# A transformer kernel's two FFNs in panels of 1024 columns, with two of eight pairs of k tiles as seven block products

## The chip, the core and the metric

The kernel runs on one core of one Trainium2 chip. Its time is the device time of one execution in microseconds (us), and the figure used is the median of several runs.

## What is computed

Two blocks in a row work on 256 tokens of 2048 numbers. Each begins with its own mixers (state space and sparse attention in the first; gated delta net and sparse attention in the second), which the change leaves alone. Each ends in the same FFN, 2048 to 8192 and back, in float32:

```python
u = rmsnorm(x, g_mlp) @ w_up
return x + jnp.square(jax.nn.relu(u)) @ w_down
```

## The kernel before

Every large product with a weight goes through `panel`. It makes a panel of 512 output columns for all 256 tokens (two token tiles, t = 0 and 1, one PSUM bank each, tiles `mm0` and `mm1`). The activations are the stationary operand, transposed, 128 of the 2048 contracted numbers (one k tile) by 128 tokens; the weights are streamed. To keep float32 accuracy with the float32r format, both operands are split in a high and a low part, and each product is three matmuls: high by high (L192), high by low (L193), low by high (L194).

Weights come in loads of 1 MB (`wst`, three buffers) on SP's queue (L201). For every 128 x 1024 elements ACT writes the high part `whi` (L207) and DVE then the low part `wlo` (L208). Each has four buffers; one holds the weights of 12 matmuls, and a buffer is free again when these 12 are done.

`ffn` (L266) has four stages of 2048 hidden columns. A stage makes four up panels and four down panels of 512 columns. After an up panel ACT takes the ReLU out of PSUM (`u`, L276), DVE squares it (L277), PE transposes it in eight steps into two `tp` banks (L287), and `split` (L170 on ACT, L172 on DVE) makes the parts `hTh` and `hTl` that the down panels use. After a down panel DVE adds each bank to the residual `X`, scaled by the squared norm factor `rr` (L292). PSUM has eight banks, in four tags of two: `mm0`, `mm1`, `tp`, `sx`. So a panel uses two banks, the next one the other two.

The order on each engine is set when the program is built: a scheduler takes the instructions of the code and interleaves them; at run time each engine follows its list strictly.

## Time and profile before

| What | us |
|---|---|
| median of three runs | 2679.77 |
| lowest and highest run | 2679.11, 2683.38 |
| span of the profiled execution, first to last instruction | 2681.1 |
| busy PE, DVE, ACT in that span | 2661.9, 1551.4, 1245.3 |
| granted TensorE clock, mean | 0.998 of full speed |

The profile gives no separate time of the profiled execution; its span is 1.3 us above the median of the runs. Busy time of PE counts overlapping matmuls once, and a matmul's row is longer than its distance to the next. An idle time in a row is that of the engine just before the instruction, with what ended it.

### The profile page before, as it was taken

The numbers are of one execution on the slowest core, as the hardware profiler recorded it, in microseconds if no ns is written. First come the engines' busy times: TensorE is split into PE (matmuls) and PEld (weight loads), VectorE is DVE, ScalarE is ACT, GpSimd is POOL, SyncE is SP. The second block draws the span as 40 slices with busy tenths as digits, with TensorE's granted clock in tenths as the row PEclk, the third lists the DMA queues.
The fourth block names the chain that finished last, engine by engine and source line by source line (L and its number), as shares of the span: only waits on it lengthen the run. The fifth ranks groups of instructions, "written<-read, shape, count | busy, mean of one in ns | idle before, by whom it ended". The sixth has DMA issues, their size and how long they took to land.

```text
span 2681.1 us, 31989 instructions
## 1 busy us (share of the span) xinstructions
PE 2661.9 (99%) x12836; PEld 2223.4 (83%) x12836; DVE 1551.4 (58%) x2023; ACT 1245.3 (46%) x1622; POOL 38.3 (1%) x46
## 2 busy tenths in 40 slices
PE   8999999999999999999999999999999999999998
PEld 8988888888888888888888877888888888888887
DVE  5767755555555555576755866455555555555554
ACT  5555544434444344454533654444444344443443
POOL 0000000000000000000100000000000000000000
PEclk9999999999999999999999999999999999999999
DMA  7444555555555655653422743556555555555564
GB/s 235 152 161 160 181 185 184 189 193 184 189 192 184 195 186 192 204 186 117 141 96 87 268 143 110 189 187 220 188 188 185 193 189 188 188 188 189 188 204 141
DMA packets 253587, 478.61 MB, mean 179 GB/s; under 512 B 9127, under 2 KB 50046, under 8 KB 253438
## 3 DMA queue, kind: packets, MB, share of 16 engines
q1 hardware_dynamic: 247280, 467.57, 52.4%
q10 hardware_dynamic: 6158, 8.99, 1.1%
q8 instruction: 101, 1.65, 0.3%
q14 instruction: 48, 0.39, 0.0%
HBM read 472.32 MB, written 4.21 MB: 178 GB/s over the span
## 4 chain that ended last, share of the span: by engine, by line
PE 98%; ACT 0%; DVE 0%; DMA 0%; issue 0%; ACTq 0%; POOL 0%; POOLq 0%; SPq 0%; DVEq 0%
PE mm L194 29%; PE mm L193 29%; PE mm L192 29%; PE tp L287 1%; PE sx L858 1%; PE sx L853 1%; PE tp L253 1%; PE tp L752 0%; PE sx L1132 0%; PE sx L887 0%; PE sx L392 0%; PE tp L545 0%; PE sx L1164 0%; PE sx L886 0%; PE mm L994 0%; PE sx L823 0%
## 5 line engine op out<-in xcount | busy, mean ns | idle before, releaser
L208 DVE TENSOR_TENSOR wlo<-wst,whi 128x1024 fp32r<-128x1024 f32 (+5 forms) x896 | 1064.0, 1189 | 956.6 <-ACT whi L207 955.4
L207 ACT ACTIVATE whi<-wst 128x1024 fp32r<-128x1024 f32 (+5 forms) x896 | 923.7, 1032 | 1181.8 <-PE mm L194 1168.8
L192 PE MATMUL mm<-whi,xnh 128*128 128x512 f32 (+3 forms) x1440 | 553.6, 385 | 2.0 <-ACT whi L207 1.6
L193 PE MATMUL mm<-wlo,xnh 128*128 128x512 f32 (+3 forms) x1440 | 552.6, 384 | 0.0
L194 PE MATMUL mm<-whi,xnl 128*128 128x512 f32 (+3 forms) x1440 | 549.9, 383 | 0.1
L193 PE MATMUL mm<-wlo,hTh 128*128 128x512 f32 x1024 | 399.4, 390 | 0.0
L192 PE MATMUL mm<-whi,hTh 128*128 128x512 f32 x1024 | 399.3, 390 | 0.0
L194 PE MATMUL mm<-whi,hTl 128*128 128x512 f32 x1024 | 398.8, 389 | 0.0
L192 PEld LDWEIGHTS mm<-whi,xnh 128*128 128x128 f32 x1440 | 270.9, 188 | 48.3 <-ACT whi L207 2.0
L194 PEld LDWEIGHTS mm<-whi,xnl 128*128 128x128 f32 x1440 | 270.9, 188 | 46.3 <-DVE xnl L174 0.4
L193 PEld LDWEIGHTS mm<-wlo,xnh 128*128 128x128 f32 x1440 | 271.3, 188 | 44.2
L193 PE MATMUL mm<-wlo,x2h 128*128 128x512 f32 (+3 forms) x736 | 278.9, 379 | 0.7 <-DVE wlo L208 0.7
L194 PE MATMUL mm<-whi,x2l 128*128 128x512 f32 (+3 forms) x736 | 279.3, 380 | 0.0
L192 PE MATMUL mm<-whi,x2h 128*128 128x512 f32 (+3 forms) x736 | 278.8, 379 | 0.0
L192 PEld LDWEIGHTS mm<-whi,hTh 128*128 128x128 f32 x1024 | 192.3, 188 | 39.7
L194 PEld LDWEIGHTS mm<-whi,hTl 128*128 128x128 f32 x1024 | 192.3, 188 | 39.6
L193 PEld LDWEIGHTS mm<-wlo,hTh 128*128 128x128 f32 x1024 | 192.3, 188 | 39.1
L193 PEld LDWEIGHTS mm<-wlo,x2h 128*128 128x128 f32 x736 | 138.9, 189 | 21.0 <-DVE wlo L208 1.0
L192 PEld LDWEIGHTS mm<-whi,x2h 128*128 128x128 f32 x736 | 138.9, 189 | 20.2 <-issue 1.1
L194 PEld LDWEIGHTS mm<-whi,x2l 128*128 128x128 f32 x736 | 138.8, 189 | 19.9 <-issue 0.9
L276 ACT ACTIVATE u<-mm 128x512 f32<-128x512 f32 x64 | 38.3, 598 | 34.0 <-PE mm L194 31.3
L277 DVE TENSOR_TENSOR u<-u 128x512 f32<-128x512 f32 x64 | 43.9, 692 | 11.3 <-ACT u L276 11.3
(411 smaller groups left out, 2131.9 us busy)
## 6 DMA issues: line engine op xcount, KB each, us to landing
wst<-in_w_up_dram SPq DMA_DIRECT2D x128, 1024.0 KB, 5.4
wst<-in_w_down_dram SPq DMA_DIRECT2D x128, 1024.0 KB, 5.0
wst<-in_w_in_dram SPq DMA_DIRECT2D x84, 1024.0 KB, 4.9
wst<-in_w_out_dram SPq DMA_DIRECT2D x16, 1024.0 KB, 5.0
wst<-in_w_o_dram SPq DMA_DIRECT2D x16, 1024.0 KB, 5.0
wst<-in_w_in_dram SPq DMA_DIRECT2D x16, 780.0 KB, 4.3
wst<-in_w_in_dram SPq DMA_DIRECT2D x12, 824.0 KB, 4.5
wst<-in_w_in_dram SPq DMA_DIRECT2D x12, 736.0 KB, 6.0
```

Source lines behind the costliest of these rows:

```text
L192: PE.matmul(ps[t][:, :n], xh[:, sl], wa, start=kt == first, stop=False)
L193: PE.matmul(ps[t][:, :n], xh[:, sl], wb, start=False, stop=False)
L194: PE.matmul(ps[t][:, :n], xl[:, sl], wa, start=False, stop=kt == last)
L207: S.activation(a[:, :2 * n], src, AF.Copy)
L208: V.tensor_tensor(b[:, :2 * n], src, a[:, :2 * n].bitcast(F32), op=OP.subtract)
L253: PE.transpose(ps[:, kk, t, :], x[:, t, (k0 + kk) * 128:(k0 + kk + 1) * 128], ident)
L276: S.activation(u, ps[t], AF.Relu)
L277: V.tensor_tensor(u, u, u, op=OP.mult)
L287: PE.transpose(pv[:, kk, t, :], us[t][:, c:c + 128], ident)
L853: PE.matmul(ps[:, i * 64:(i + 1) * 64].rearrange("p (m b) -> p m b", b=b), N[:, i], half(T[:, i], 0), start=True, stop=True)
L858: PE.matmul(ps[:, i * 64:(i + 1) * 64].rearrange("p (m b) -> p m b", b=b), P[:, i], half(Tt[:, i], 1), start=True, stop=True)
```

## The change

In both FFNs, `wide` takes the place of `panel` for 1024 columns at once. A load of 1 MB now holds two k tiles by 1024 columns, in rows of 4 KB instead of 2 KB. Each pair of k tiles, with two token tiles and two halves of 512 columns, is a 2 x 2 by 2 x 2 block product. In six of the eight pairs it is done as before by eight products of three matmuls. In pairs 2 and 5 (`SPAIRS`) it is done by seven products, by Winograd's form of Strassen's algorithm: sums of activation blocks (`a_forms`, made once per activation) by sums of weight blocks (`t13`, `t24`, made on DVE for each load). A panel holds eight banks: P2, P3, P4, E take the plain pairs and some of the seven; P1, P5, P6, P7 only take products of pairs 2 and 5, and `shared` adds them up on ACT and DVE. The two groups of tags change roles from panel to panel. The last two 512-column down panels of each FFN stay in the old form, so there are 15 wide panels in an FFN.

After an up panel DVE adds each of P2, P3, P4, E to its shared part (new line L376), ACT takes the ReLU, now with the norm factor as scale (L377), and ACT squares it (L378). The transposes are L390. `s2` has one buffer more.

```diff
@@ -218,6 +218,98 @@
             mms(*m)
         return ps
 
+    SPAIRS = (2, 5)
+    turn = [0]
+    def a_forms(f, forms, j):
+        sf = s2([128, 4, 128], name="sf")
+        V.tensor_tensor(sf[:, 0], f[:, 0, 1], f[:, 1, 1], op=OP.add)
+        V.tensor_tensor(sf[:, 2], f[:, 0, 0], f[:, 0, 1], op=OP.subtract)
+        V.tensor_tensor(sf[:, 1], sf[:, 0], f[:, 0, 0], op=OP.subtract)
+        V.tensor_tensor(sf[:, 3], f[:, 1, 0], sf[:, 1], op=OP.subtract)
+        sh, sl = s2([128, 4, 128], F32R, "sfh"), s2([128, 4, 128], F32R, "sfl")
+        split(flat(sf), flat(sh), flat(sl))
+        forms[j] = sh, sl
+    def wide(w, r0, c0, lhs, forms):
+        ka, kb = (("mm0", "mm1"), ("tp", "sx"))[::1 - 2 * (turn[0] % 2)]
+        turn[0] += 1
+        B = {}
+        for k, names in zip((ka[0], ka[1], kb[0], kb[1]), (("P2", "P3"), ("P4", "E"), ("P1", "P5"), ("P6", "P7"))):
+            for b in names:
+                B[b] = psum(k, [128, 512])
+        ns = len(SPAIRS)
+        left = {b: 3 * ns + (0 if b in ("P1", "P5", "P6", "P7") else 6 * (8 - ns)) for b in B}
+        left["E"] = 6 * (8 - ns)
+        total = dict(left)
+        def mm(b, x, y):
+            PE.matmul(B[b], x, y, start=left[b] == total[b], stop=left[b] == 1)
+            left[b] -= 1
+        def product(b, xh, xl, wa, wb):
+            mm(b, xh, wa)
+            mm(b, xh, wb)
+            mm(b, xl, wa)
+        def parts(src, n=1024):
+            a = whp.tile([128, 1024], F32R, name="whi")
+            b = wlp.tile([128, 1024], F32R, name="wlo")
+            S.activation(a[:, :n], src, AF.Copy)
+            V.tensor_tensor(b[:, :n], src, a[:, :n].bitcast(F32), op=OP.subtract)
+            return [(a[:, o:o + 512], b[:, o:o + 512]) for o in range(0, n, 512)]
+        for j in range(8):
+            s = stp.tile([128, 2048], F32, name="wst")
+            nc.sync.dma_start(s.rearrange("p (k n) -> p k n", k=2),
+                              w[r0 + j * 256:r0 + j * 256 + 256, c0:c0 + 1024].rearrange("(k p) n -> p k n", p=128))
+            if j not in SPAIRS:
+                for kk in range(2):
+                    xh, xl = lhs(2 * j + kk)
+                    wl = parts(s[:, kk * 1024:(kk + 1) * 1024])[::-1]
+                    for i, l, b in ((0, 0, "P2"), (0, 1, "P3"), (1, 0, "P4"), (1, 1, "E")):
+                        h = slice(i * 128, i * 128 + 128)
+                        product(b, xh[:, h], xl[:, h], *wl[l])
+                continue
+            t13 = sp([128, 2, 512], name="t13")
+            V.tensor_tensor(t13, s.rearrange("p (k l n) -> p k l n", k=2, l=2)[:, :, 0],
+                            s[:, :1024].rearrange("p (l n) -> p l n", l=2)[:, ::-1], op=OP.subtract)
+            t24 = sp([128, 2, 512], name="t24")
+            V.tensor_tensor(t24[:, 0], s[:, 1024:1536], t13[:, 0], op=OP.subtract)
+            V.tensor_tensor(t24[:, 1], s[:, 1536:], t24[:, 0], op=OP.subtract)
+            (a1h, a1l), (a2h, a2l) = lhs(2 * j), lhs(2 * j + 1)
+            m1, m2 = slice(0, 128), slice(128, 256)
+            sh, sl = forms[j]
+            def sums(n):
+                return sh[:, n - 1], sl[:, n - 1]
+            w11, w22 = parts(s[:, 512:1536])
+            product("P1", a1h[:, m1], a1l[:, m1], *w11)
+            product("P3", *sums(4), *w22)
+            u1, u3 = parts(flat(t13))
+            product("P5", *sums(1), *u1)
+            product("P7", *sums(3), *u3)
+            u2, u4 = parts(flat(t24))
+            product("P6", *sums(2), *u2)
+            product("P4", a2h[:, m2], a2l[:, m2], *u4)
+            (w21,) = parts(s[:, 1536:], 512)
+            product("P2", a2h[:, m1], a2l[:, m1], *w21)
+        return B, ka
+    def shared(B):
+        p1, u2, u4, v = (s2([128, 512], name=n) for n in ("cp1", "cu2", "cu4", "cv"))
+        S.activation(p1, B["P1"], AF.Copy)
+        V.tensor_tensor(u2, B["P6"], p1, op=OP.add)
+        V.tensor_tensor(u4, B["P5"], u2, op=OP.add)
+        V.tensor_tensor(u2, B["P7"], u2, op=OP.add)
+        V.tensor_tensor(v, B["P5"], u2, op=OP.add)
+        return ((0, 0, p1, B["P2"]), (0, 1, u4, B["P3"]), (1, 0, u2, B["P4"]), (1, 1, v, B["E"]))
...
@@ -244,16 +336,27 @@
             start += z
         return o
 
-    def x_to_act(x, q, gain):
-        """One [128 tokens, 2, 512] panel of x -> [128, 4, 256] transposed, times gain, in two parts."""
+    def x_to_act(x, q, gain, forms=None, p=0):
         for k0 in range(0, 4, 2):
             ps = psum("tp", [128, 512]).rearrange("p (k t c) -> p k t c", k=2, t=2)
             for kk in range(2):
                 for t in range(2):
                     PE.transpose(ps[:, kk, t, :], x[:, t, (k0 + kk) * 128:(k0 + kk + 1) * 128], ident)
+            if forms is not None and 2 * p + k0 // 2 in SPAIRS:
+                f = s2([128, 2, 2, 128], name="ff")
+                for kk in range(2):
+                    S.activation(f[:, kk], ps[:, kk], AF.Copy, scale=gain[:, k0 + kk:k0 + kk + 1])
+                f_to_act(f, q, k0, forms, 2 * p + k0 // 2)
+                continue
             for kk in range(2):
                 k = k0 + kk
                 split(ps[:, kk].rearrange("p t c -> p (t c)"), q[0][:, k], q[1][:, k], gain[:, k:k + 1])
+    def f_to_act(f, q, k0, forms, j):
+        fv = f.rearrange("p k t c -> p (k t c)")
+        split(fv, flat(q[0][:, k0:k0 + 2]), flat(q[1][:, k0:k0 + 2]))
+        a_forms(f, forms, j)
 
     def x_rstd(ssx, name):
         ss = tiny([128, 2], "ssr")
@@ -263,37 +366,57 @@
     def flat(ap):
         return ap.rearrange("p k c -> p (k c)")
 
-    def ffn(X, act, w_up, w_down, r, after, tail=0):
-        rr = tiny([128, 2], "rr")
-        V.tensor_tensor(rr, r, r, op=OP.mult)
+    def ffn(X, act, forms, w_up, w_down, r, after, tail=0):
         for s_ in range(4):
-            hT = []
-            for p in range(4):
-                ps = panel(w_up, 0, 16, s_ * 2048 + p * 512, 512, at_k(act))
-                us = []
-                for t in range(2):
-                    u = s2([128, 512], name=f"u{t}")
-                    S.activation(u, ps[t], AF.Relu)
-                    V.tensor_tensor(u, u, u, op=OP.mult)
-                    us.append(u)
-                q = quarter("hT")
-                hT.append(q)
-                for k0 in range(0, 4, 2):
-                    pt = psum("tp", [128, 512])
-                    pv = pt.rearrange("p (k t c) -> p k t c", k=2, t=2)
-                    for kk in range(2):
+            hT, hforms = [], {}
+            for P in range(2):
+                B, tags = wide(w_up, 0, s_ * 2048 + P * 1024, at_k(act), forms)
+                us = {}
+                for i, l, part, bank in shared(B):
+                    V.tensor_tensor(part, bank, part, op=OP.add)
+                    S.activation(part, part, AF.Relu, scale=r[:, i:i + 1])
+                    S.activation(part, part, AF.Square)
+                    us[i, l] = part
+                for l in (1, 0):
+                    q = quarter("hT")
+                    p = len(hT)
+                    hT.append(q)
+                    for k0 in range(0, 4, 2):
+                        pt = psum(tags[k0 // 2], [128, 512])
+                        pv = pt.rearrange("p (k t c) -> p k t c", k=2, t=2)
+                        for kk in range(2):
+                            for t in range(2):
+                                c = (k0 + kk) * 128
+                                PE.transpose(pv[:, kk, t, :], us[t, l][:, c:c + 128], ident)
+                        j = 2 * p + k0 // 2
+                        if j in SPAIRS:
+                            f = s2([128, 2, 2, 128], name="ff")
+                            S.activation(f.rearrange("p k t c -> p (k t c)"), pt, AF.Copy)
+                            f_to_act(f, q, k0, hforms, j)
+                        else:
+                            split(pt, flat(q[0][:, k0:k0 + 2]), flat(q[1][:, k0:k0 + 2]))
+            for P in range(2):
+                if (s_, P) == (3, 1):
+                    for p in (2, 3):
+                        ps = panel(w_down, s_ * 2048, 16, p * 512, 512, at_k(hT), tail=tail if p == 3 else 0)
                         for t in range(2):
-                            c = (k0 + kk) * 128
-                            PE.transpose(pv[:, kk, t, :], us[t][:, c:c + 128], ident)
-                    split(pt, flat(q[0][:, k0:k0 + 2]), flat(q[1][:, k0:k0 + 2]))
-            for p in range(4):
-                ps = panel(w_down, s_ * 2048, 16, p * 512, 512, at_k(hT), tail=tail if (s_, p) == (3, 3) else 0)
-                for t in range(2):
-                    V.scalar_tensor_tensor(X[p][:, t], ps[t], rr[:, t:t + 1], X[p][:, t], op0=OP.mult, op1=OP.add)
-                    if s_ == 3:
-                        after(p, t)
-
```

The lists of the engines change most where an up panel ends and the next panel begins. In the rows below a tile's name ends in its own number, and `whi_4079` is one buffer's worth of weights.

ACT, end of an up panel, before (the two ReLUs of the panel stand between the splits for the next one):

```order
L207 ACTIVATE whi_3977<-wst_3959 128x1024
L207 ACTIVATE whi_3995<-wst_3993 128x1024
L276 ACTIVATE u0_3935<-mm0_3797 128x512
L276 ACTIVATE u1_3938<-mm1_3798 128x512
L207 ACTIVATE whi_4011<-wst_3993 128x1024
L170 ACTIVATE hTh_3941<-tp_3943 128x512
L170 ACTIVATE hTh_3941<-tp_3950 128x512
L207 ACTIVATE whi_4029<-wst_4027 128x1024
```

and now, at the end of the first up panel (`cp1`, `cu4`, `cu2`, `cv` are the four quarters of u):

```order
L261 ACTIVATE whi_4045<-wst_4027 128x1024
L261 ACTIVATE whi_4063<-wst_4061 128x1024
L377 ACTIVATE cp1_3955<-cp1_3955,r2_3651 128x512
L261 ACTIVATE whi_4079<-wst_4061 128x1024
L378 ACTIVATE cp1_3955<-cp1_3955 128x512
L377 ACTIVATE cu4_3957<-cu4_3957,r2_3651 128x512
L377 ACTIVATE cu2_3956<-cu2_3956,r2_3651 128x512
L378 ACTIVATE cu4_3957<-cu4_3957 128x512
L378 ACTIVATE cu2_3956<-cu2_3956 128x512
L377 ACTIVATE cv_3958<-cv_3958,r2_3651 128x512
L261 ACTIVATE whi_4102<-wst_4095 128x1024
L378 ACTIVATE cv_3958<-cv_3958 128x512
```

Two instructions per 512 columns became eight per 1024, four of which read what another one of ACT has just written, and a split of weights for the next panel stands between the first ReLU and its square, another one ahead of the last square.

DVE at the same place, before:

```order
L208 TENSOR_TENSOR wlo_3996<-wst_3993,whi_3995 128x1024
L277 TENSOR_TENSOR u0_3935<-u0_3935 128x512
L277 TENSOR_TENSOR u1_3938<-u1_3938 128x512
L208 TENSOR_TENSOR wlo_4012<-wst_3993,whi_4011 128x1024
L172 TENSOR_TENSOR hTl_3942<-tp_3943,hTh_3941 128x512
L172 TENSOR_TENSOR hTl_3942<-tp_3950,hTh_3941 128x512
L208 TENSOR_TENSOR wlo_4030<-wst_4027,whi_4029 128x1024
L208 TENSOR_TENSOR wlo_4046<-wst_4027,whi_4045 128x1024
```

and now:

```order
L262 TENSOR_TENSOR wlo_4030<-wst_4027,whi_4029 128x1024
L310 TENSOR_TENSOR cv_3958<-tp_3660,cu2_3956 128x512
L262 TENSOR_TENSOR wlo_4046<-wst_4027,whi_4045 128x1024
L279 TENSOR_TENSOR t13_4097<-wst_4095 128x1024
L376 TENSOR_TENSOR cp1_3955<-mm0_3655,cp1_3955 128x512
L376 TENSOR_TENSOR cu4_3957<-mm0_3656,cu4_3957 128x512
L376 TENSOR_TENSOR cu2_3956<-mm1_3657,cu2_3956 128x512
L376 TENSOR_TENSOR cv_3958<-mm1_3658,cv_3958 128x512
L262 TENSOR_TENSOR wlo_4064<-wst_4061,whi_4063 128x1024
L262 TENSOR_TENSOR wlo_4080<-wst_4061,whi_4079 128x1024
L282 TENSOR_TENSOR t24_4099<-wst_4095,t13_4097 128x512
L283 TENSOR_TENSOR t24_4099<-wst_4095,t24_4099 128x512
```

The two squares are gone. In their place are four adds that read the banks, behind the difference `t13_4097` of the next panel's third load (`wst_4095`).

PE, just after the end of an up panel, before (`mm0_3797`, `mm1_3798` are the next panel):

```order
L192 MATMUL mm1_3798<-whi_3801,xnh_3119 128x512
L287 MATMUL tp_3783<-idt_82,u0_3775 128x128
L287 MATMUL tp_3790<-idt_82,u0_3775 128x128
L193 MATMUL mm1_3798<-wlo_3802,xnh_3119 128x512
L194 MATMUL mm1_3798<-whi_3801,xnl_3120 128x512
L287 MATMUL tp_3783<-idt_82,u1_3778 128x128
L287 MATMUL tp_3783<-idt_82,u0_3775 128x128
L287 MATMUL tp_3783<-idt_82,u1_3778 128x128
L287 MATMUL tp_3790<-idt_82,u1_3778 128x128
L287 MATMUL tp_3790<-idt_82,u0_3775 128x128
L287 MATMUL tp_3790<-idt_82,u1_3778 128x128
L192 MATMUL mm0_3797<-whi_3801,xnh_3119 128x512
```

and now (`tp_4020` is the next panel; five products stand ahead of these rows, and two more and six transposes follow, four of them of `cv` and two of `cu4`):

```order
L250 MATMUL tp_4020<-whi_4045,xnh_3119 128x512
L250 MATMUL tp_4020<-wlo_4046,xnh_3119 128x512
L250 MATMUL tp_4020<-whi_4045,xnl_3120 128x512
L390 MATMUL mm0_3978<-idt_82,cu4_3957 128x128
L390 MATMUL mm1_3985<-idt_82,cu4_3957 128x128
L390 MATMUL mm0_3994<-idt_82,cp1_3955 128x128
L390 MATMUL mm0_3994<-idt_82,cu2_3956 128x128
L390 MATMUL mm0_3994<-idt_82,cp1_3955 128x128
L390 MATMUL mm0_3994<-idt_82,cu2_3956 128x128
L390 MATMUL mm1_4012<-idt_82,cp1_3955 128x128
L390 MATMUL mm1_4012<-idt_82,cu2_3956 128x128
L390 MATMUL mm1_4012<-idt_82,cp1_3955 128x128
```

The first transposes stood behind four matmuls of the next panel; they now stand behind 18.

## Rows read from the trace of the kernel before

**Rows 1.** The page: busy time, granted clock, one group of matmuls.
```profile
PE 2661.9 (99%) x12836; PEld 2223.4 (83%) x12836; DVE 1551.4 (58%) x2023; ACT 1245.3 (46%) x1622; POOL 38.3 (1%) x46
...
PEclk9999999999999999999999999999999999999999
...
L192 PE MATMUL mm<-whi,hTh 128*128 128x512 f32 x1024 | 399.3, 390 | 0.0
```
**Rows 2.** What PE waited for, whole span: total us, times, longest.
```profile
PE tp L141 <- DMA P<-in_g_mix_dram: 5.3, 1, 5.3
PE mm L193 <- DVE wlo L208: 0.7, 1, 0.7
```
**Rows 3.** Timeline of PE, start and us: two matmuls, 54 apart, steady.
```profile
2008.43 0.39 PE L192 MATMUL mm<-whi,xnh 128*128 128x512 f32 x1
...
2020.67 0.39 PE L192 MATMUL mm<-whi,xnh 128*128 128x512 f32 x1
```
**Rows 4.** One up panel with its eight transposes, busy time by engine.
```profile
2004.29:2027.10 22.81, 22.81 (x106) 18.72 (x105) 12.37 (x13) 10.66 (x13) 0.00 (x0) 1.00 0.57 186
```
**Rows 5.** Groups by form on DVE and ACT: xcount | busy us, mean ns.
```profile
L208 DVE TENSOR_TENSOR wlo<-wst,whi 128x1024 fp32r<-128x1024 f32 x776 | 949.9, 1225 | 883.4 <-ACT whi L207 882.5 <-issue 0.2
...
L277 DVE TENSOR_TENSOR u<-u 128x512 f32<-128x512 f32 x64 | 43.9, 692 | 11.3 <-ACT u L276 11.3
...
L172 DVE TENSOR_TENSOR hTl<-tp,hTh 128x512 fp32r<-128x512 f32 x64 | 41.0, 682 | 0.0
...
L838 DVE TENSOR_TENSOR N<-A,C 128x512 f32<-128x512 f32 x20 | 13.7, 684 | 0.0
...
L483 DVE TENSOR_TENSOR NP<-sx,Bt 128x512 f32<-128x512 f32 x8 | 5.5, 685 | 1.1 <-PE sx L1132 0.9
...
L817 DVE SCALAR_TENSOR_TENSOR D<-D,rk,C 128x128 f32<-128x128 f32 x16 | 4.5, 344 | 0.0
...
L207 ACT ACTIVATE whi<-wst 128x1024 fp32r<-128x1024 f32 x776 | 822.3, 1060 | 1064.0 <-PE mm L194 1053.5 <-DMA wst<-in_w_in_dram 3.0 <-issue 2.6
...
L276 ACT ACTIVATE u<-mm 128x512 f32<-128x512 f32 x64 | 38.3, 598 | 34.0 <-PE mm L194 31.3
...
L170 ACT ACTIVATE hTh<-tp 128x512 fp32r<-128x512 f32 x64 | 34.8, 596 | 15.6 <-PE tp L287 15.6
...
L1055 ACT ACTIVATE gsq<-O 128x512 f32<-128x512 f32 x4 | 2.3, 616 | 0.0
...
L1231 ACT ACTIVATE X<-X,r 128x512 f32<-128x512 f32 x2 | 1.4, 724 | 2.1 <-POOL r L159 2.1
```
**Rows 6.** Timeline at the end of an up panel: start, us, engine.
```profile
2002.82 1.28 ACT L276 ACTIVATE u<-mm 128x512 f32<-128x512 f32 x2 [0.98 <-PE mm L194]
...
2003.45 1.37 DVE L277 TENSOR_TENSOR u<-u 128x512 f32<-128x512 f32 x2 [0.35 <-ACT u L276]
...
2003.99 1.06 ACT L207 ACTIVATE whi<-wst 128x1024 fp32r<-128x1024 f32 x1
...
2004.29 0.41 PE L287 MATMUL tp<-idt,u 128*128 128x128 f32 x2
```
**Rows 7.** Timeline inside a panel: matmul, next weight split on ACT, DVE.
```profile
2009.79 0.39 PE L192 MATMUL mm<-whi,xnh 128*128 128x512 f32 x1
...
2009.99 1.06 ACT L207 ACTIVATE whi<-wst 128x1024 fp32r<-128x1024 f32 x1 [1.68 <-PE mm L194]
...
2011.08 1.23 DVE L208 TENSOR_TENSOR wlo<-wst,whi 128x1024 fp32r<-128x1024 f32 x1 [1.51 <-ACT whi L207]
```
**Rows 8.** Weight loads: queue, median us to landing, min/median/max in 2000:2600.
```profile
q1 hardware_dynamic: 247280, 467.57, 52.4%
...
wst<-in_w_up_dram SPq DMA_DIRECT2D x128, 1024.0 KB, 5.4
...
wst<-in_w_down_dram SPq DMA_DIRECT2D x128, 1024.0 KB, 5.0
...
DMA to landing us min/median/max: 4.9/5.4/7.7
```
**Rows 9.** Timeline of ACT: a Copy (L207) and a Square (L167) behind it.
```profile
1957.97 1.06 ACT L207 ACTIVATE whi<-wst 128x1024 fp32r<-128x1024 f32 x1 [1.66 <-PE mm L194]
...
1958.94 0.61 ACT L167 ACTIVATE junk<-X 128x512 bf16<-128x512 f32 x1
```

More of the change, by code (lines that the diff above doesn't have):

```diff
@@ L71, in build @@
     drp = ctx.enter_context(tc.tile_pool(name="drp", bufs=1, space=bass.MemoryType.DRAM))
-    NP, N4, N2, N1 = 7, 17, 15, 5
+    NP, N4, N2, N1 = 7, 17, 16, 5
     def sp(shape, dt=F32, name="sp"):
@@ new lines, in ffn @@
+            for P in range(2):
+                if (s_, P) == (3, 1):
+                    for p in (2, 3):
+                        ps = panel(w_down, s_ * 2048, 16, p * 512, 512, at_k(hT), tail=tail if p == 3 else 0)
+                        for t in range(2):
+                            V.tensor_tensor(X[p][:, t], ps[t], X[p][:, t], op=OP.add)
+                            after(p, t)
+                    continue
+                B, _ = wide(w_down, s_ * 2048, P * 1024, at_k(hT), hforms)
+                out_ = shared(B)
+                for i, l, part, bank in out_:
+                    x = X[2 * P + 1 - l][:, i]
+                    V.tensor_tensor(x, part, x, op=OP.add)
+                for i, l, part, bank in out_:
+                    x = X[2 * P + 1 - l][:, i]
+                    V.tensor_tensor(x, bank, x, op=OP.add)
+                if s_ == 3:
+                    for p in range(2):
+                        for t in range(2):
+                            after(p, t)
@@ L660, in build, with add_panel @@
     ssx = tiny([128, 2, 4], "ssx", bufs=2)
-    def add_panel(ps, p, scale, act, gain, ssx):
+    def add_panel(ps, p, scale, act, gain, ssx, forms):
         for t in range(2):
@@ L665, in add_panel @@
         q = quarter("xn")
-        x_to_act(X[p], q, gain[:, 4 * p:4 * p + 4])
+        x_to_act(X[p], q, gain[:, 4 * p:4 * p + 4], forms, p)
         act.append(q)
@@ L671, in build @@
     X = x_panels()
+    xforms = {}
     for p in range(4):
@@ L689, in after1 @@
             nc.scalar.dma_start(xsave[:, p], X[p])
-    ffn(X, xn, I["w_up"][0], I["w_down"][0], r, after1)
+    ffn(X, xn, xforms, I["w_up"][0], I["w_down"][0], r, after1)
     if upto == 2:
@@ L1199, in build @@
     xn = []
+    xforms = {}
     ssx = tiny([128, 2, 4], "ssx", bufs=2)
@@ L1205, in build @@
         q = quarter("xn")
-        x_to_act(X[p], q, g_ln2[:, 4 * p:4 * p + 4])
+        x_to_act(X[p], q, g_ln2[:, 4 * p:4 * p + 4], xforms, p)
         xn.append(q)
```

4 lines of the change are left out of this document (2 added, 2 removed).

## The prediction

> **What bounds the kernel now.** I read the page first. PE is busy 99% of the span at a granted clock of nine tenths or more in all 40 slices, DVE 58%, ACT 46% [rows 1]. A busy PE need not be a limiting one, since a matmul's row (390 ns) overlaps the next. So the second view is what PE waited for: the longest wait is 5.3 us for the first load, and inside the panels nothing above 0.7 us is listed [rows 2]. The third is PE's timeline: 54 matmuls of a panel take 2020.67 - 2008.43 = 12.24 us, 0.2267 us each, without a gap [rows 3]. The bound is therefore the number of matmuls times 0.2267 us. The reader should see the reverse on the other engines: ACT's weight split starts 0.20 us after the slot of the last matmul that used its buffer, having sat idle 1.68 us, and DVE's half follows 1.09 us later, after 1.51 us idle [rows 7]. ACT and DVE wait for PE, four buffers ahead of it.
>
> **What is removed.** An FFN has 15 wide panels (eight up, seven down). Each leaves out one product of three matmuls in two pairs: 30 x 2 x 3 = 180 matmuls, x 0.2267 = **40.8 us**. The form of the other matmuls is the same. The transposes stay, 16 per 1024 columns; eight cost 22.81 - 96 x 0.2267 = 1.05 us now [rows 4], and I leave that.
>
> **What is added on DVE and ACT, in total.** Durations are from [rows 5]; where an operation is new, the nearest form stands for it (SBUF adds 0.684, adds with a bank 0.685, 128 x 128 blocks at most 0.344, ReLU with a scale from SBUF 0.724, square from SBUF 0.616). For an up panel DVE has 18 full splits and two half ones (23.4 us), the weight sums t13 and t24 (2 x 2.6), four shared and four bank adds (5.5), four hTl (2.7), one set of forms (1.9): 38.7 us. PE takes 186 x 0.2267 + 2.1 = 44.3 us. DVE goes from 12.37 of 22.81 us [rows 4] to 87%. ACT has 29.9 us, 67%. Neither is the bound on average, so the question is where it is late.
>
> **A pair of seven.** PE needs 21 x 0.2267 = 4.76 us, DVE 3 x 1.225 + 0.69 + 2.6 = 7.0. Cover is the buffers. During the two plain pairs ahead (10.88 us) DVE has to make two tiles and all of the pair's, 2.45 + 7.0 = 9.5: 1.4 us to spare. Behind the pair, the first tile is free after six matmuls, at 1.36 + 0.20, ready 1.09 + 1.23 us later [rows 7], at 3.9, and needed at 4.76: 0.9 to spare. I price both at nothing; without cover, each of the 60 pairs would pay what is missing.
>
> **The end of an up panel.** This is where I expect the loss. Now the chain is two ReLUs, two squares, transposes [rows 6]: the two ReLUs start at 2002.82 and the first transposes run at 2004.29, behind four matmuls of the next panel, with hardly a hole. Afterwards (ACT's list above) the ReLUs and squares of all four quarters and two weight splits go through ACT in a row. Count from the end of the last matmul's slot. The split of `whi_4079` waits for that buffer, 0.20, and ends at 1.26; square of cp1 1.88, two ReLUs 3.32, squares of cu4 3.94 and cu2 4.56, ReLU of cv 5.28, the split of `whi_4102` 6.34, square of cv 6.96. PE asks for cu4 after 18 matmuls, at 4.08, for cu2 at about 4.4, for cv at about 6.7 (ten transposes and six matmuls on). Behind a waiting transpose stand the next panel's matmuls. Lost: about 0.45 us even with nothing late.
>
> Something is late, though. DVE's bank adds stand behind `t13_4097`, which reads the next panel's third load. Its buffer is that of the ending panel's last load. DVE is done with that after three back-to-back splits from about -11.1 (tile free at -12.5, ACT's 1.06, one add of 0.69), so at -7.4. A load lands 5.0 to 5.4 us after its issue (medians), at worst 7.7 [rows 8], so at -2.4; but the load before it was issued 2.45 earlier and lands at -4.8, and the queue's 52.4% of 2681.1 us for 467.57 MB makes 3.15 us of transfer per load, so -1.65. Then t13 ends at -0.4, the add of cp1 at 0.3, its ReLU at 1.0, and the split that should start at 0.20 starts at 1.0. All of the chain moves by 0.85: 1.3 us lost. The bounds are 0.45 (rows of 4 KB land earlier than those of 2 KB; no row shows them) and 0.45 + 0.85 + 2.7 = 4.0 (each landing like the worst row). I take 1.2, near the medians: 16 up panels x 1.2 = **19 us back**.
>
> A down panel has no transposes; its adds must be done before those banks are written again, at pair 2 of the next panel, 10.9 us on, and eight adds take 5.5. I price that at nothing. At the head of each FFN the second product needs the bank of the panel before, an add of about 0.7 us, partly covered: 1 us for both.
>
> Moving the square to ACT costs no table change that the trace shows: a Square starts 0.97 us after a Copy of 1.06 us began, without a pause [rows 9]. Per instruction it gains little: 692 ns on DVE, 616 on ACT [rows 5]. The Trainium skill (ScalarE: Activation LUTs, Rules for kernel authors) says the opposite of this edit: use VectorE, not ScalarE, for relu and mul. The trace disagrees on the price for these float32 tiles, 692 against 616 ns. By that rule the four squares belong on DVE, which would shorten ACT's chain by 4 x 0.62 and put 2.8 us on DVE; it changes the size of the 19 us, not its sign.
>
> **Sum.** 2681.1 - 40.8 + 19 + 1 = 2660.3 for a profiled span; the runs stand 1.3 lower, so **2659 us**.
>
> **Rivals.** *All covers hold.* Loads land early enough that t13 never waits; 0.45 x 16 = 7 us come back: 2681.1 - 40.8 + 7 + 1 - 1.3 = 2647. For it: bigger rows. Against: two loads close together on one queue.
>
> *The third load lands late* (slower than before). Every us beyond 5.0 goes one to one into DVE's adds, ACT's chain and PE. The gain is gone at 39.8 / 16 = 2.5 us per up panel, a landing at about 6.2; at 6.5 the time is 2681.1 - 40.8 + 45 + 1 - 1.3 = 2685, at 7.7 it is 2704. For it: the maximum of [rows 8], and that loads now come in bunches. Against: the medians.
>
> *DVE starves PE at the pairs of seven.* With 0.9 and 1.4 us to spare over 87% load, a hold-up of a little over 1 us on DVE shows. At 0.3 us per pair, 18 us: 2677. For it: the adds that read PSUM stand among the splits in DVE's list. Against: between pairs 3 and 4 nothing else stands there.
>
> *Every panel end has a hole.* All eight banks belong to one panel now, and so nothing is double-buffered; if the next panel's first products wait for banks at down panels too, 30 holes of 1.2 us make 36: 2681.1 - 40.8 + 36 + 1 - 1.3 = 2676. Against: in DVE's list the add of cv, the last to read P1, P5, P6 or P7, stands ahead of the last split that the next panel's first pair needs. The Trainium skill (Trainium Kernel Development and Optimization, Best Practices) says to mind PSUM pressure and that consistent bubbles can mean PSUM ran out; by that rule this rival's hole is the one to look for.
>
> That the matmuls left out don't count is excluded by [rows 2, 3].
>
> **Chances.** Forecast (2652 to 2667) 0.45; covers hold 0.25; late load 0.09; DVE starves 0.13; hole at each panel 0.08. Two in ten are left out of 2642 to 2679. What a measurement can tell from no change is 0.2%, 5.4 us. Below 2674.4 lie the first two and part of the third to fifth: faster 0.83; same 0.10; slower 0.07.
>
> **What the profile would show.** Right: PE has 180 matmuls fewer at 0.227 us apart; the wait of PE for ACT's squares at the transposes is near 1.2 us in each of 16 places and little else is waited for; DVE's first bank add starts after t13, which waits for its load. Wrong, if weight splits (`whi`, `wlo`) top PE's waits, if bank adds delay products of the next panel, or if the transposes wait longer than 2.5 us.

## The result, and the profile of the changed kernel

The changed kernel takes 2651.02 us (median of 4 runs, 2646.3 to 2654.01); the kernel before takes 2679.83 beside it. The ratio is 0.9886, with a 95% interval of 0.9872 to 0.99: 1.1% faster. The profiled execution has a span of 2652.2 us. The forecast was 2659, so the time came out 8 us better than forecast, between the likeliest case and the rival in which all covers hold (2647). It lies 1 us under the band of 2652 to 2667 that the prediction gave 0.45, and inside its wider one of 2642 to 2679. Executions of the kernel before took 2678.9 to 2679.9 us with a mean granted clock of 0.999 and 2681.8 to 2684.1 with 0.998, so a median moves by up to 3 us with how many it has of either.

In the text TensorE is the PE of the rows, VectorE is DVE and ScalarE is ACT; SP issues the loads.

From the page of the changed kernel come the busy times and the queue of the weight loads, against [rows 1, 8]:

```profile
PE 2623.1 (99%) x12656; PEld 2195.1 (83%) x12656; DVE 1917.3 (72%) x2593; ACT 1411.5 (53%) x1876; POOL 39.2 (1%) x46
...
q1 hardware_dynamic: 185840, 467.57, 52.3%
```

TensorE has 12836 - 12656 = 180 matmuls fewer, the number that the prediction counted. VectorE does 366 us more than before and ScalarE 166 more, and PE is still busy 99% of the span: the added work lies beside the matmuls. The loads carry the same bytes in fewer packets.

What PE waited for in the changed kernel, against [rows 2] (total us, times, longest):

```profile
PE tp L390 <- ACT cu L378: 5.3, 4, 1.7
...
PE mm L390 <- ACT cu L378: 4.5, 5, 1.5
...
PE mm L193 <- DVE wlo L208: 0.8, 1, 0.8
```

The first two rows are one wait, split by the bank that is written: the first transposes behind an up panel (L390) wait for ScalarE's square of u (L378). It is 9.8 us in 9 of the 16 up-panel ends. The weight splits of the FFN (L261, L262) do not appear at all.

The groups by form of the new operations, against [rows 5] (xcount | busy us, mean ns | idle before, and what ended it):

```profile
L279 DVE TENSOR_TENSOR t<-wst 128x1024 f32<-128x1024 f32 x60 | 73.2, 1221 | 26.1 <-DMA wst<-in_w_down_dram 17.3 <-DMA wst<-in_w_up_dram 8.8
...
L378 ACT ACTIVATE cu<-cu 128x512 f32<-128x512 f32 x32 | 18.2, 616 | 0.0
...
L377 ACT ACTIVATE cp<-cp,r 128x512 f32<-128x512 f32 x16 | 11.6, 725 | 32.7 <-DVE cp L376 32.7
```

The durations are those that the prediction took from neighbouring forms (t13 1221 ns, square 616, ReLU 725). What matters is in the idle columns: t13 (L279) waits 26.1 us for loads, and the first ReLU of each panel (L377 on cp) 32.7 us for VectorE's addition.

The timeline of the changed kernel at one up panel's end where the load is late, and at one where it is nearly in time (start, us, engine; idle before it in brackets):

```profile
437.75 0.37 SPq L267 DMA_DIRECT2D wst<-in_w_up_dram  x1
...
440.56 3.49 DVE L262 TENSOR_TENSOR wlo<-wst,whi 128x1024 fp32r<-128x1024 f32 x3
...
441.80 0.37 SPq L267 DMA_DIRECT2D wst<-in_w_up_dram  x1
...
444.07 0.37 SPq L267 DMA_DIRECT2D wst<-in_w_up_dram  x1
...
451.52 0.39 PE L250 MATMUL mm<-whi,xnl 128*128 128x512 f32 x1
...
451.61 1.23 DVE L279 TENSOR_TENSOR t<-wst 128x1024 f32<-128x1024 f32 x1 [2.78 <-DMA wst<-in_w_up_dram]
...
452.75 0.68 DVE L376 TENSOR_TENSOR cp<-mm,cp 128x512 f32<-128x512 f32 x1
...
453.53 0.72 ACT L377 ACTIVATE cp<-cp,r 128x512 f32<-128x512 f32 x1 [3.24 <-DVE cp L376]
...
454.16 1.04 ACT L261 ACTIVATE whi<-wst 128x1024 fp32r<-128x1024 f32 x1
...
457.53 0.44 PE L390 MATMUL mm<-idt,cu 128*128 128x128 f32 x2 [1.53 <-ACT cu L378]
...
2033.90 1.23 DVE L279 TENSOR_TENSOR t<-wst 128x1024 f32<-128x1024 f32 x1 [1.27 <-DMA wst<-in_w_down_dram]
...
2039.40 0.39 PE L250 MATMUL tp<-whi,hTl 128*128 128x512 f32 x1
...
2039.76 0.44 PE L390 MATMUL mm<-idt,cu 128*128 128x128 f32 x2
```

The chain is the one that the prediction described: t13 waits for the third load of the next panel, the bank additions stand behind it, then ReLU, a weight split and squares on ScalarE, then the transposes. At 451.61 the load is 2.78 us late and PE loses 1.53; at 2033.90 it is 1.27 late and no wait of PE is listed. Read so, the nine ends with a loss have waits of t13 of 1.50 to 3.05 us and losses of 0.20 to 1.74, each 1.25 to 1.31 smaller than its wait; where t13 waited 1.27 or less, no wait is listed. So PE loses what the load is late beyond about 1.3 us, which is the cover of this order. (The brackets count from the end of the last matmul's row, 0.39 us behind its start, while matmuls start 0.2267 apart. At 2039.76 the transposes start 0.36 behind the last matmul, where at an end with the load in time it is 0.23 (2514.88 and 2515.11), so about 0.13 is lost without a bracket, and each of the nine losses is about 0.16 more than listed.)

The upper rows show how the load comes late. The matmul at 451.52 is the last of the ending panel. The first three issues on SP's queue are the next panel's first three loads. VectorE does three splits back to back (440.56, 3.49 us), which frees two buffers 2.27 us apart; the third load is issued at 444.07, while the second is still moving, and lands 7.5 us later, at 451.6. The close issue does not by itself make a load late: at the nine ends with a loss t13 starts 6.3 to 7.8 us behind the issue of its load, at the other seven, where the issues are 2.27 us apart too, 5.0 to 6.0. Seven of the nine late loads are of the down weights (the 17.3 us above are the waits for eight of these, the 8.8 those for the eight of the up weights); why these come later is not shown.

### The profile page after: what moved, and what is told of

Same layout as the page of the kernel before. It is cut to its first block, busy times and chain, and to the rows that moved or that the text cites. A ratio compares the mean times of both kernels' runs of the same rounds, so it can differ in the third digit from the quotient of the medians.

```text
span 2652.2 us, 32498 instructions
## 1 busy us (share of the span) xinstructions
PE 2623.1 (99%) x12656; PEld 2195.1 (83%) x12656; DVE 1917.3 (72%) x2593; ACT 1411.5 (53%) x1876; POOL 39.2 (1%) x46
## 3 DMA queue, kind: packets, MB, share of 16 engines
q8 instruction: 99, 1.62, 0.2%
## 4 chain that ended last, share of the span: by engine, by line
PE 92%; DMA 3%; DVE 2%; ACT 2%; issue 1%; ACTq 0%; POOL 0%; POOLq 0%; SPq 0%; DVEq 0%
PE mm L250 21%; PE mm L193 13%; PE mm L194 13%; PE mm L192 13%; PE tp L250 11%; PE sx L250 10%; DMA wst<-in_w_down_dram 2%; DVE wlo L262 2%; PE sx L982 1%; ACT whi L261 1%; PE sx L977 1%; PE tp L345 1%; PE mm L390 1%; DMA wst<-in_w_up_dram 1%; PE tp L876 0%
## 5 line engine op out<-in xcount | busy, mean ns | idle before, releaser
L208 DVE TENSOR_TENSOR wlo<-wst,whi 128x1024 fp32r<-128x1024 f32 (+6 forms) x416 | 475.8, 1147 | 321.6 <-ACT whi L207 320.7
L261 ACT ACTIVATE whi<-wst 128x1024 fp32r<-128x1024 f32 x480 | 476.8, 1005 | 379.3 <-PE mm L250 164.1
L207 ACT ACTIVATE whi<-wst 128x1024 fp32r<-128x1024 f32 (+6 forms) x416 | 414.7, 998 | 467.4 <-PE mm L194 437.2
L262 DVE TENSOR_TENSOR wlo<-wst,whi 128x1024 fp32r<-128x1024 f32 x480 | 543.5, 1155 | 140.7 <-ACT whi L261 133.1
L261 ACT ACTIVATE whi<-t 128x1024 fp32r<-128x1024 f32 x120 | 127.3, 1061 | 150.5 <-PE mm L250 76.8
L262 DVE TENSOR_TENSOR wlo<-t,whi 128x1024 fp32r<-128x1024 f32 x120 | 146.9, 1224 | 80.1 <-ACT whi L261 79.7
L192 PE MATMUL mm<-whi,xnh 128*128 128x512 f32 (+3 forms) x416 | 153.0, 369 | 2.0 <-ACT whi L207 1.6
L193 PE MATMUL mm<-wlo,xnh 128*128 128x512 f32 (+3 forms) x416 | 152.2, 366 | 0.0
L194 PE MATMUL mm<-whi,xnl 128*128 128x512 f32 (+3 forms) x416 | 150.9, 366 | 0.1
L250 PE MATMUL mm<-whi,hTh 128*128 128x512 f32 x378 | 148.4, 393 | 0.0
L250 PE MATMUL mm<-wlo,hTh 128*128 128x512 f32 x378 | 147.7, 391 | 0.0
L250 PE MATMUL mm<-whi,hTl 128*128 128x512 f32 x378 | 147.5, 390 | 0.0
```

What stands on the lines that cost most here:

```text
L192: PE.matmul(ps[t][:, :n], xh[:, sl], wa, start=kt == first, stop=False)
L193: PE.matmul(ps[t][:, :n], xh[:, sl], wb, start=False, stop=False)
L194: PE.matmul(ps[t][:, :n], xl[:, sl], wa, start=False, stop=kt == last)
L207: S.activation(a[:, :2 * n], src, AF.Copy)
L208: V.tensor_tensor(b[:, :2 * n], src, a[:, :2 * n].bitcast(F32), op=OP.subtract)
L250: PE.matmul(B[b], x, y, start=left[b] == total[b], stop=left[b] == 1)
```

## The experiments

Theory 1: what comes back of the saving is the late third load, met by t13 on VectorE ahead of the panel's bank additions. Theory 2: ScalarE's chain of ReLU and square, with all eight banks in one panel, makes the transposes wait whatever the loads do. Theory 3: VectorE has too much to do and its splits come late. A fourth buffer for the loads, which would attack the lateness itself, was not tried.

Times are medians of runs with the kernel before beside them on the same chip, and the ratio is to that kernel. e1 to e9 ran on one chip, e10 on another.

| kernel | pairs by seven products | us (lowest to highest) | ratio, 95% interval |
|---|---|---|---|
| changed | 3rd, 6th | 2651.0 (2646.3 to 2654.0) | 0.9886 (0.9872 to 0.99) |
| e1 | 4th, 7th | 2646.3 (2645.7 to 2647.7) | 0.9866 (0.9852 to 0.9879) |
| e2 | 4th, 6th | 2641.5 (2638.1 to 2642.4) | 0.9845 (0.9831 to 0.9858) |
| e4 | 3rd, 6th, square on VectorE | 2650.9 (2650.6 to 2652.6) | 0.9883 (0.987 to 0.9897) |
| e5 | none | 2681.1 (2680.0 to 2682.2) | 0.9994 (0.9985 to 1.0003) |
| e6 | 3rd, 6th, t13 from other data | 2648.6 (2647.2 to 2651.1) | 0.988 (0.9865 to 0.9895) |
| e7 | 3rd | 2661.0 (2659.3 to 2664.4) | 0.9927 (0.9912 to 0.9942) |
| e8 | 6th | 2660.2 (2659.3 to 2660.5) | 0.9922 (0.9907 to 0.9936) |
| e9 | 4th, 6th, t24 computed twice | 2641.0 (2640.5 to 2641.3) | 0.985 (0.9833 to 0.9866) |
| e10 | 3rd, 5th | 2641.8 (2639.5 to 2643.5) | 0.9852 (0.9835 to 0.9868) |

### e2 and e1: other pairs, so that t13 stands behind the bank additions

```diff
-    SPAIRS = (2, 5)
+    SPAIRS = (3, 5)
```

> The pairs of seven are the fourth and sixth, so only one of them moves against the changed kernel; the third split stands behind the bank additions too. Theory 1: as with the fourth and seventh, transposes' wait below 2 us and 2640 (2636 to 2645). Theory 2: wait near 10 us, 2651. Theory 3: the two pairs of seven stand one pair nearer to each other, their splits crowd more than with the fourth and seventh, and TensorE waits within the panel: 2655 or more, and above the run with the fourth and seventh.

For e1, `SPAIRS = (3, 6)`:

> The pairs of seven are the fourth and seventh instead of the third and sixth, so at a wide up panel's end VectorE no longer meets the third split (the one whose load can be late) ahead of the panel's bank additions. Theory 1 (the late load, met ahead of the additions, is what comes back of the saving): TensorE's wait for the first transposes, 9.8 us in the changed kernel, falls below 2 us, the fall of the granted clock behind it goes too, and the time is about 11 us under the changed kernel's 2651: 2640, in 2636 to 2645. Theory 2 (the chain of addition, ReLU and square, with all eight banks in use, makes the wait whatever the loads do): the wait stays near 10 us and the time at 2651. Theory 3 (VectorE has too much to do): splits that now stand behind the additions come late, TensorE waits for them within the panels by 1 us or more each, and the time is 2655 or more.

e2 came out at 2641.5 with the same number of matmuls, 9.5 us below the changed kernel (11 by the ratios). What PE waited for in e2, its timeline at the same panel's end, and the time to landing of the load issued at 443.99:

```profile
PE tp L141 <- DMA P<-in_g_mix_dram: 5.3, 1, 5.3
PE mm L192 <- ACT whi L207: 1.6, 1, 1.6
PE mm L193 <- DVE wlo L208: 1.5, 2, 0.8
```

```profile
441.72 0.37 SPq L267 DMA_DIRECT2D wst<-in_w_up_dram  x1
...
443.99 0.37 SPq L267 DMA_DIRECT2D wst<-in_w_up_dram  x1
...
449.88 0.69 DVE L376 TENSOR_TENSOR cp<-mm,cp 128x512 f32<-128x512 f32 x1 [1.08 <-PE mm L250]
...
450.66 0.73 ACT L377 ACTIVATE cp<-cp,r 128x512 f32<-128x512 f32 x1 [0.40 <-DVE cp L376]
...
454.81 0.44 PE L390 MATMUL mm<-idt,cu 128*128 128x128 f32 x2
```

```profile
DMA to landing us min/median/max: 6.7/6.7/6.7
```

The wait for the squares is gone from the list. The reader sees in the brackets what VectorE's addition waits for now: PE, its producer, and no longer a load. The loads crowd as before: the third is issued 2.27 us behind the second and lands 6.7 us later, at 450.7, when the first addition has begun. Only t13 no longer stands in front. Theory 2, that ScalarE's chain with all banks in use makes the wait by itself, is out: the same operations and the same banks are here, and from the first addition to the transposes it is 454.81 - 449.88 = 4.93 us, against 457.53 - 452.75 = 4.78 in the changed kernel.

e1 has no wait for the squares either, but lands 4.8 us above e2. Its list names part of that:

```profile
PE mm L193 <- DVE wlo L208: 2.6, 3, 1.5
...
PE mm L192 <- DVE X L413: 0.8, 1, 0.8
```

These are 1.9 us more than in e2, of 3.4 between the two spans (2643.7 and 2640.3). Another 0.5 is one wait of a transpose in the mixers (L1266). The rest was not traced to a place.

### e5: the wide panels and the square on ScalarE alone

`SPAIRS = ()`, `shared` with its additions left out, and the down panels' additions of the shared parts left out too:

```diff
-                    V.tensor_tensor(part, bank, part, op=OP.add)
-                    S.activation(part, part, AF.Relu, scale=r[:, i:i + 1])
+                    part = s2([128, 512], name="u")
+                    S.activation(part, bank, AF.Relu, scale=r[:, i:i + 1])
                     S.activation(part, part, AF.Square)
```

> The wide panels and the square on ScalarE stay, but all eight pairs are computed by eight products: 180 matmuls more, no partial sums, no bank additions ahead of the ReLU. It tells what the wide panel and the square are worth alone. Theory 1: the wide panel costs nothing by itself, and with no additions between a late split and the ReLU the transposes do not wait: 2680 less the measured 2651 gives the seven products' net worth, so this run comes at the kernel before's time, 2680, in 2674 to 2686. Theory 2 (all eight banks of a panel end together and cost a wait at every end): 2690 or more. Theory 3: VectorE has less to do than in both kernels; TensorE's waits are the smallest of all, 2672 to 2680.

The ratio is 0.9994 (0.9985 to 1.0003): wide panels, one load per two k-tiles and the square on ScalarE change nothing that is measured. The whole gain belongs to the products left out. It also gives the floor: 2681.1 - 40.8 = 2640.3, against 2641.5 for e2. Next to nothing of the 40.8 is lost there.

### e4: the square back on VectorE

```diff
-                    S.activation(part, part, AF.Square)
+                    V.tensor_tensor(part, part, part, op=OP.mult)
```

> The square of u is back on VectorE, all else as in the changed kernel. The square's 0.62 us leaves ScalarE's chain and its 0.6 to 0.7 comes behind the bank additions on VectorE. Theory 1: the third split still waits for its load ahead of the additions; the transposes wait still grows one to one with its lateness, with a cover that is 1.3 us plus or minus about 0.5: a few us either way, 2648 to 2654. Theory 2 (the ScalarE chain makes the wait): without a square in the chain the wait falls below 3 us whatever the load, 2642. Theory 3 (VectorE is near its bound): 32 squares of 0.69 us per FFN more on it, TensorE waits for splits, 2660 or more.

2650.9, the time of the changed kernel, where theory 2 had 2642. The waits only change their name:

```profile
PE tp L390 <- DVE cu L378: 5.2, 5, 1.4
PE mm L390 <- DVE cu L378: 3.1, 5, 1.2
```

8.3 us now for VectorE's squares. Taking 0.62 us out of ScalarE's chain for each square helped little; the addition behind the late load stayed where it was.

### e8 and e7: one pair alone

> Only the sixth pair of each wide panel is computed by seven products: 90 of the 180 matmuls are back, and no third split reads a late load ahead of a panel's bank additions. Theory 1: half the saving in full, 90 x 0.2267 = 20.4 us under the 2681.1 of the wide panels with no pair of seven: 2660.7, in 2658 to 2664; the transposes after an up panel do not wait. Theory 2 (bank additions, ReLU and square make the wait by themselves): they are all here too, so about 10 us of waits and 2670.

> Only the third pair is computed by seven products. As many matmuls as with the sixth alone, but the difference of the third load again stands on VectorE ahead of the bank additions. Theory 1: the same 20.4 us less, and the waits at the up panels' ends come back: 2660.7 plus 4 to 10 us, 2665 to 2671, with the wait of the transposes equal to the wait of that difference for its load less 1.3 us, panel by panel. Theory 2: the same time as with the sixth pair alone, within 2 us.

The sixth pair alone (`SPAIRS = (5,)`) met the expectation: 20.9 us below e5, half of the saving in full. No wait for the squares is in its list, although its third loads are issued 2.3 us behind the second as in the changed kernel. The time to landing of the latest of them, issued at 1015.38:

```profile
DMA to landing us min/median/max: 8.7/8.7/8.7
```

The third alone (`(2,)`) did not: 2661.0, 20.1 below e5, where 2665 to 2671 had been expected. Its list of waits has 3.5 us for the squares, a little less than the 4 to 10 expected:

```profile
PE tp L390 <- ACT cu L378: 2.1, 3, 1.6
...
PE mm L390 <- ACT cu L378: 1.4, 1, 1.4
```

The median hides part of this: two of e7's runs, with a mean granted clock of 0.999, took 2659.3, the two with 0.998 took 2662.7 and 2664.4, and e8's four all had 0.998. Theory 2 had e7 within 2 us of e8, which the medians are; but it had put e8 at 2670, so it stays out. Added up, 2681.1 - 20.9 - 20.1 = 2640.1 would follow for both; the changed kernel takes 2651.0. In ratios, which take the chips out, 0.9994 - 0.0072 - 0.0067 = 0.9855 against 0.9886, 8 us. So most of the loss exists only when the two stand together, 8 to 11 us by these sums and 9.8 against 3.5 and none by the lists of waits, and theory 1 as I had put it ("the place ahead of the additions costs") was incomplete. The timeline of e7 shows what is different, at the panel end of 451.61 above and at a later one:

```profile
437.91 0.37 SPq L267 DMA_DIRECT2D wst<-in_w_up_dram  x1
...
443.35 0.37 SPq L267 DMA_DIRECT2D wst<-in_w_up_dram  x1
...
448.68 1.22 DVE L279 TENSOR_TENSOR t<-wst 128x1024 f32<-128x1024 f32 x1
...
625.65 1.23 DVE L279 TENSOR_TENSOR t<-wst 128x1024 f32<-128x1024 f32 x1 [1.40 <-DMA wst<-in_w_up_dram]
...
631.64 0.44 PE L390 MATMUL mm<-idt,cu 128*128 128x128 f32 x2 [1.36 <-ACT cu L378]
```

The third load (443.35) is issued 5.44 us after the second (437.91) instead of 2.27, and t13 does not wait for it at 448.68: no bracket stands behind it. Where a load was late all the same (625.65), PE lost 1.36 of 1.40 us: in e7 a weight split (627.39, 1.22 us) stands between the first and the second addition, and next to no cover is left. So t13's place decides whether PE pays for a late load, and the sixth pair has a large part in whether the load is late.

### e10: the sixth pair moved to the fifth

```diff
-    SPAIRS = (2, 5)
+    SPAIRS = (2, 4)
```

> The third and fifth pairs by seven products. The difference of the third load stands ahead of the bank additions as in the changed kernel, but the other pair of seven lies one pair earlier, so that three plain pairs follow it in the panel. In the changed kernel the buffers for the second and third loads of the next panel come free 2.3 us apart (5.4 us apart with the third pair alone), and the third load takes up to 7.5 us instead of 5. Theory 1, as it stands now (the third load is late because two loads are issued close together behind the sixth pair's bunch of splits): the issues are 4 to 5.5 us apart again, the difference waits little, the transposes wait under 4 us in all, and the time is 2641 to 2646. Theory 1 as first stated (the place ahead of the additions alone is what costs): waits near 10 us, 2651.

2641.8, in the range of theory 1 as it then stood, and 9 us below the place-alone theory. Its timeline at the same panel end, and its row of waits:

```profile
436.12 0.37 SPq L267 DMA_DIRECT2D wst<-in_w_up_dram  x1
...
438.39 0.37 SPq L267 DMA_DIRECT2D wst<-in_w_up_dram  x1
...
443.22 0.37 SPq L267 DMA_DIRECT2D wst<-in_w_up_dram  x1
...
448.55 1.22 DVE L279 TENSOR_TENSOR t<-wst 128x1024 f32<-128x1024 f32 x1
...
449.72 0.69 DVE L376 TENSOR_TENSOR cp<-mm,cp 128x512 f32<-128x512 f32 x1
```

```profile
PE tp L390 <- ACT cu L378: 1.3, 3, 0.6
```

t13 still stands ahead of the additions. The 2.27 us between two issues have moved to the first and second load; the third comes 4.83 after the second, and t13 at 448.55 waits for nothing. Where t13 waits in e10 (four ends, 0.16 to 0.58 us) PE loses all but 0.03 of it, so this order has no cover either, and what it gains is that the loads come in time. Between the changed kernel, e2 and e10 both halves of the cause have been taken away one at a time, and each removal brings the time to within 2 us of the floor.

### e6: t13 of the up panels from data already in SBUF

```diff
-            V.tensor_tensor(t13, s.rearrange("p (k l n) -> p k l n", k=2, l=2)[:, :, 0],
-                            s[:, :1024].rearrange("p (l n) -> p l n", l=2)[:, ::-1], op=OP.subtract)
+            x13 = (s.rearrange("p (k l n) -> p k l n", k=2, l=2)[:, :, 0],
+                   s[:, :1024].rearrange("p (l n) -> p l n", l=2)[:, ::-1])
+            if j == 2 and w.shape[1] > 2048:
+                x13 = [f.rearrange("p k c -> p (k c)").bitcast(F32)[:, None, :].to_broadcast([128, 2, 512])
+                       for _, f in (forms[2], forms[5])]
+            V.tensor_tensor(t13, *x13, op=OP.subtract)
```

> The changed kernel, but in the up panels the first difference of the third pair is made from data that is already in SBUF (the low parts of two activation sums), so the products of that pair are not the reference's. VectorE then does that difference long before the panel's end, and what meets the load ahead of the bank additions is the next operation, 0.69 us long instead of 1.22. Theory 1: the additions start when the load has landed and that operation is done, 0.53 us earlier, so the cover grows from 1.3 to about 1.8 us; by the nine waits of the changed kernel, 9.8 - 9 x 0.53 = 5 us of them are left, and 2646 (2644 to 2649). Theory 2: the waits stay at 10 us, 2651. A third way, that only the first difference is dangerous: no waits, 2641.

2648.6, inside theory 1's range and near its upper end, but the experiment is weaker than its expectation. It touches the eight ends behind which another up panel follows, and only two of the nine that waited are among these. There the order on PE moved too:

```profile
450.05 0.69 DVE L286 TENSOR_TENSOR t<-wst,t 128x512 f32<-128x512 f32 x1 [1.72 <-DMA wst<-in_w_up_dram]
...
453.87 0.44 PE L394 MATMUL mm<-idt,cu 128*128 128x128 f32 x2 [0.64 <-ACT cu L382]
```

At the touched end the transposes run 3.8 us behind the operation that waits, instead of 5.9, and the cover is 1.72 - 0.64 = 1.1, not the 1.8 that I had expected. At the untouched end that follows, where t13 starts at 495.19 and the transposes at 501.04, 2.01 - 0.70 = 1.3 holds again. It neither proves nor harms the theory.

### e9: how much slack VectorE has

```diff
             V.tensor_tensor(t24[:, 1], s[:, 1536:], t24[:, 0], op=OP.subtract)
+            V.tensor_tensor(t24[:, 0], s[:, 1024:1536], t13[:, 0], op=OP.subtract)
+            V.tensor_tensor(t24[:, 1], s[:, 1536:], t24[:, 0], op=OP.subtract)
```

> The fourth and sixth pairs by seven products (2641.5), and in each of the 60 such pairs the second difference's two halves are computed twice over, with the same data: 1.38 us more on VectorE per pair, 83 us in all. It measures the slack that the prediction read off as 0.9 and 1.4 us per pair. Theory 1 as the prediction had it: the slack just holds, or 0.5 us per pair comes through at worst: 2642 to 2665. VectorE near its bound (the rival): the splits come late at every pair, 60 x 1 us or more, 2700.

2641.0 against e2's 2641.5. The page of e9 shows that the work was done:

```profile
PE 2619.6 (99%) x12656; PEld 2192.5 (83%) x12656; DVE 1986.5 (75%) x2713; ACT 1413.5 (54%) x1876; POOL 40.6 (2%) x46
```

VectorE is busy 68 us longer than in e2 (1918.3), in 120 more instructions, and PE does not notice. That is 68 / 60 = 1.1 us for each pair, less than the 1.38 expected. The rival of a starved PE needs more than this on top of each pair in this order.

## Why the prediction was right, and where it was off

**The bound and the saving.** Right. PE was bound by its number of matmuls, and 180 fewer are worth 40.8 us: e2 shows 39.6 of them against e5.

**The additions on VectorE and ScalarE, the square and the wide panels at nothing.** Right: e5 (0.9994) for the wide form and the square, e4 for the square once more, e9 for the slack at the pairs. The Trainium skill (ScalarE: Activation LUTs, Rules for kernel authors) would have the square on VectorE, as the prediction weighed; in e4 that is 2650.9 against 2651.0, no difference either way, since neither engine bounds the kernel.

**The end of an up panel.** The mechanism was the one forecast: t13 ahead of the bank additions, waiting for the next panel's third load, and the delay going one to one through ScalarE's chain to the transposes. The size was not. The prediction had "about 0.45 us even with nothing late" and 0.85 of lateness at every end, 1.2 x 16 = 19 us. Measured are 9.8 us of waits at nine ends, up to 1.74, and none at seven. Two terms were off, one too high and one too low, and that they cancel in part is luck.

The step that failed is the 0.45: with nothing late there is no loss but cover. I had laid durations end to end, while successive rows of an engine overlap: the addition starts at 452.75, before t13's 451.61 + 1.23 = 452.84 is over, and the split at 454.16 before the ReLU's 453.53 + 0.72 = 454.25. The Trainium skill (ScalarE: Activation LUTs, What ACT_TABLE_LOAD costs) says that successive operations on ScalarE overlap by some 93 ns; the trace agrees, with 0.09 us between ScalarE's two rows, and shows 0.09 between VectorE's two as well. The prediction's own [rows 9] had shown it, with a Square 0.97 us behind the start of a Copy of 1.06. Over the split, the square, two ReLUs and the square that precede the transposes, my count was 3.94 - 0.20 = 3.74 us; the rows have 457.53 - 454.16 = 3.37. So the square of cu4 is ready about 0.5 us before PE asks for it, not 0.14 (4.08 - 3.94). The listed times do not give 0.45 either, but 0.26: cu2 is 4.56 - 4.4 = 0.16 late and cv 6.96 - 6.7 = 0.26, and the first of these waits puts off the asking for cv. The rest of the cover of 1.3 lies ahead of the split, which cannot start before its buffer is free; that part the prediction had counted.

The 0.85 was too low where a load is late and too high elsewhere. The last slot of the ending panel is over at 451.52 + 0.23 = 451.75; 0.20 behind it, at 451.95, the split could start, and it starts at 454.16, 2.2 us late.

**The load.** It was sized by medians of landing (5.0 to 5.4 us) and by queueing behind the load before it, and so was to land 5.75 us after its issue (from -7.4 to -1.65). Both were on the right track: at the nine ends the third load takes 6.3 to 7.8 us, issued 2.27 us behind the second (2.45 in the prediction). What the prediction did not see is that this closeness comes from the other pair of seven. Moving the sixth pair takes the closeness away (e10); moving the third leaves it, and takes t13 out of its way (e2).

**The heads of the FFNs.** 1 us was given for the second product's bank. No such wait is in PE's list; nothing was lost there.

**The rivals.** *DVE starves PE* and *a hole at every panel* are out: neither weight splits of the FFN nor banks of down panels are among PE's waits. The Trainium skill's rule on PSUM pressure (Trainium Kernel Development and Optimization, Best Practices) was behind the second; no bubble of that kind is in this trace. *The third load lands late* is what happens at nine ends, all of them beyond its 6.2 us, but not at its price: the loss is 9.8 / 16 = 0.6 us per up panel, not 2.5. Its 6.2 counts from 5.0, although the forecast itself had the load at 5.75, and it has no cover. *All covers hold* is not the changed kernel, where t13 does wait; e2 and e10, where PE hardly waits, show what it would have been, 2641 to 2642 and not 2647, since its 7 us were the same wrong 0.45.

**The sum again.** The 19 became 9.8 of waits and 1.6 for a fall of the clock behind one of them (last section), and the 1 for the heads nothing: 8.6 us less than summed, and 8 less were measured. Between profiled executions it is e5's span of 2678.9 - 40.8 + 9.8 + 1.6 = 2649.5, against 2652.2. Of the 2.7 left, 9 x 0.16 = 1.5 is what the brackets leave out; an estimate of 1.7 more comes from the mixers, where the granted clock is 0.50 for 6.8 us in the changed kernel (from 1564.1) and for 3.4 in e5 (from 1574.7). The 1.3 taken off for the runs holds for no execution by itself: the profiled one of the changed kernel has a span of 2652.2 and took 2654.0, 1.8 more.

## What to carry to other kernels

An engine that executes in order passes the lateness of a load on to everything behind it: before placing an early operation on a new load ahead of a producer that PE needs, ask when that load's buffer comes free, and what else is issued in the 2 to 3 us before it. Two edits that cost little apart (none and 3.5 us of waits) can cost more together (9.8) when one makes loads crowd and the other waits for them; moving either by one step gave the whole gain (e2, e10: 2641.5 and 2641.8). When a chain of short operations is added up for a cover of about 1 us, the small overlap of successive rows decides between a loss and none, so take start-to-start times from a timeline where it has them.
